# Running the second half of a gated embedding behind the last expert, tile by tile

## The chip, the cores and the metric

The kernel runs on one core of one Trainium2 chip. The metric is the device time of one execution in microseconds (us); a kernel's time is the median of its runs. Five engines work side by side: PE (matmuls, with PEld for the loads of its stationary operand), DVE, ACT, POOL and SP. SP issues nearly all weight loads. POOL issues the transfers that gather, scatter or add, on a queue of its own. The order of work on each engine is fixed when the program is built.

## The reference, cut to what matters

Two layers; each ends with a mixture of experts, a gated embedding and a layer norm. S is 512 rows, D_MODEL 1024, D_EXPERT 256, 16 experts, of which each row uses two.

```python
def hier_moe(h, ...):
    ...                                   # gates: (512, 16), two nonzeros a row
    a = jnp.einsum('td,edf->tef', t, w1)
    c = jnp.einsum('td,edf->tef', t, w3)
    act = jax.nn.silu(a) * c * gates[:, :, None].astype(t.dtype)
    y = jnp.einsum('tef,efd->td', act, w2)
...
    for i in range(DEPTH):
        ...
        h = layer_norm(DN_ALPHA * h + mix, ln1_g[i], ln1_b[i])
        y_moe = hier_moe(h, ...)
        y_ple = jax.nn.sigmoid(h @ ple_wg[i] + ple_bg[i]) * (p[i] @ ple_wp[i])
        h = layer_norm(DN_ALPHA * h + y_moe + y_ple, ln2_g[i], ln2_b[i])
```

## The kernel before

All matrix products are made of three matmuls: each operand is split in a high part (a cast on ACT, line 224) and a low part (a subtraction on DVE, line 225), and `mm3` adds high by high, low by high and high by low. Weights are streamed as a list of units in the order of use (`plan`). A unit is up to 128x1024 floats (0.52 MB): its raw tile is loaded by SP (line 240), then split, then used. `pump` loads some units ahead and splits a few ahead (`ahead_raw`, `ahead_split`: 15 and 3 in the expert stage, 7 and 3 from expert 10 on, 8 and 4 for the last expert). Raw and split tiles come from one set of 34 slots.

The 512 rows stand in four tiles of 128. After the first layer norm each tile goes to DRAM twice: to `hd`, from which experts gather their rows, and to `yd`, to which all that is to be added is added by accumulating transfers. An expert e takes four units for its two input products (`e<-whi,xT`), then a Silu (line 1274), a product, two transposes, a split of the activations (`actT`), and two units for its output (`e<-whi,actT`). The output units of expert e stand behind the input units of expert e + 1. The result is scaled by the gate into one of two places (`ye`, line 1323) and scattered into `yd` by POOL (line 1257). Experts 14 and 15 are treated apart: their results stay in SBUF as high and low parts (`yl`, lines 1315 and 1316), and one-hot matmuls (`hotT`, line 1431) bring them to their rows in the tail.

The gated embedding has a product of 1024 by 1024 (`ple_wg`) and one of 256 by 1024 (`ple_wp`, kept as `pwp`). Its first 512 columns are computed before expert 0. The second 512 columns take four units of weights, `pl<-...`, 24 matmuls each; two units run behind expert 3 and two behind expert 12 (`PLE_AT`). Each column half ends as bias sum (line 1206), tanh (line 1207) and product with `pwp` (line 1208), and is added into `yd` by POOL (line 1228).

The tail of a layer: POOL loads the four tiles of `yd` back (`h<-yd`, line 1412). `tail_sum` adds the one-hot products (on DVE, line 1437, or, for the tiles in `ZPE`, through an identity matmul and ACT, lines 1434 and 1435) and takes the row sums; then come the mean (line 362), the squares (line 364), the root on POOL (lines 305 and 308) and the two steps of the norm (lines 348 and 350, or 334 and 336). In the first layer each normed tile is transposed and split into `hT`, and the next layer's first projections (`pj`) start on it; in the second layer it is stored as output.

## Time and profile before

| | |
|---|---|
| median of 3 runs | 1043.53 us (1042.79 to 1048.24) |
| profiled execution | 1045.37 us, of which the trace spans 1043.6 |
| busy: PE, PEld | 968.6 us (93%), 800.6 us (77%) |
| busy: DVE, ACT, POOL | 779.1 (75%), 613.6 (59%), 172.9 (17%) |
| moved by DMA | 197.49 MB, 189 GB/s over the span |

The trace is of one execution. PE's busy time overstates its load, since matmuls overlap: a matmul of 512 columns has a duration of 0.39 us, but at full pace one starts every 0.23 us. PEld is the better measure of PE's pace. Clock times below are microseconds from the start of the span; the first layer's experts run from about 341 to 522, the second layer's from about 834 to 1016.

### The profile page before, as it was taken

What the parts mean: (1) busy time and instruction counts of PE and PEld (TensorE: products, weight loads), DVE (VectorE), ACT (ScalarE), POOL (GpSimd) and SP (SyncE); (2) the same over time, 40 slices, a digit from 0 to 9 for tenths busy, and PEclk for the clock granted to TensorE, in tenths of its full rate; (3) what the DMA queues carried; (4) which work ended last, traced back from release to release, by engine and by line L of the source; (5) the groups of instructions that cost most, each with busy time, mean ns of one, the idle gap of its engine ahead of it and who ended that gap; (6) DMA issues with size and microseconds to landing.
All of it is one profiled execution on the core that took longest, in us unless ns stands there. A gap on an engine that the chain in (4) does not pass through costs nothing. (4 is left out here: it accounts for less than half of the span.)

```text
span 1043.6 us, 14416 instructions
## 1 busy us (share of the span) xinstructions
PE 968.6 (93%) x4869; PEld 800.6 (77%) x4870; DVE 779.1 (75%) x1301; ACT 613.6 (59%) x1046; POOL 172.9 (17%) x170
## 2 busy tenths in 40 slices
PE   4999999999989999999979999999998999999995
PEld 3887889898767788777758889898776778877762
DVE  7576897777676778887865578847678587888785
ACT  5425464655653768886843346654655386888673
POOL 1101000000222222422121000000012222333121
PEclk9999999999999999999989999999999999999997
DMA  8816121222974999999974412122186399999974
GB/s 262 239 37 142 51 71 52 71 81 68 316 242 102 306 302 311 307 292 301 285 261 114 109 56 67 51 70 83 61 302 243 94 329 302 315 300 312 293 207 161
DMA packets 156010, 197.49 MB, mean 189 GB/s; under 512 B 20296, under 2 KB 123786, under 8 KB 155925
## 3 DMA queue, kind: packets, MB, share of 16 engines
q1 hardware_dynamic: 135253, 155.58, 45.5%
q0 software_dynamic: 20672, 40.87, 15.1%
q8 instruction: 42, 0.69, 0.3%
q14 instruction: 43, 0.35, 0.1%
HBM read 182.85 MB, written 29.36 MB: 203 GB/s over the span
## 5 line engine op out<-in xcount | busy, mean ns | idle before, releaser
L225 DVE TENSOR_TENSOR wlo<-raw,whi 128x1024 fp32r<-128x1024 f32 (+2 forms) x278 | 324.1, 1182 | 66.0 <-ACT whi L224 61.1
L224 ACT CAST whi<-raw 128x1024 fp32r<-128x1024 f32 (+2 forms) x278 | 277.9, 1024 | 33.1 <-DMA raw<-in_moe_w_dram 13.9
L218 PE MATMUL e<-whi,xT 128*128 128x512 f32 x256 | 106.6, 416 | 2.7 <-ACT xT L224 1.8
L219 PE MATMUL e<-wlo,xT 128*128 128x512 f32 x256 | 103.7, 405 | 0.1
L220 PE MATMUL e<-whi,xT 128*128 128x512 f32 x256 | 101.8, 398 | 0.0
L218 PE MATMUL pj<-whi,hT 128*128 128x384 f32 x256 | 90.0, 352 | 2.3 <-ACT hT L224 1.8
L219 PE MATMUL pj<-wlo,hT 128*128 128x384 f32 x256 | 88.2, 345 | 0.3 <-DVE wlo L225 0.3
L220 PE MATMUL pj<-whi,hT 128*128 128x384 f32 x256 | 87.3, 342 | 0.6 <-DVE hT L225 0.5
L1257 POOL DMA_INDIRECT yd<-ye,rt_tok x28 | 53.1, 1895 | 187.2 <-ACT ye L1323 66.7
L868 ACT ACTIVATE prob<-sc,mx 128x512 f32<-128x512 f32 x64 | 43.7, 688 | 39.1 <-DVE mx L867 36.6
L308 POOL TENSOR_TENSOR ors<-rs_y,mhalf 128x4 f32<-128x4 f32 x8 | 8.5, 1057 | 335.3 <-DVE rs_y L307 335.3
L1251 POOL DMA_INDIRECT xe<-hd,rt_tok x32 | 48.8, 1525 | 91.4 <-PE tr L376 48.1
L218 PEld LDWEIGHTS e<-whi,xT 128*128 128x128 f32 x256 | 48.9, 191 | 12.9 <-ACT xT L224 2.2
L219 PEld LDWEIGHTS e<-wlo,xT 128*128 128x128 f32 x256 | 48.8, 191 | 11.4 <-DVE wlo L225 2.4
L220 PEld LDWEIGHTS e<-whi,xT 128*128 128x128 f32 x256 | 48.8, 191 | 10.0
L219 PE MATMUL e<-wlo,actT 128*128 128x512 f32 x128 | 51.6, 403 | 3.1 <-DVE wlo L225 3.1
L218 PE MATMUL mo<-whi,YT 128*128 128x512 f32 x128 | 53.2, 415 | 0.0
L218 PEld LDWEIGHTS pj<-whi,hT 128*128 128x128 f32 x256 | 48.9, 191 | 4.8 <-ACT hT L224 2.5
L219 PE MATMUL pl<-wlo,hT 128*128 128x512 f32 x128 | 51.4, 401 | 1.1 <-DVE wlo L225 1.1
L218 PE MATMUL pl<-whi,hT 128*128 128x512 f32 x128 | 50.8, 402 | 0.6 <-ACT whi L224 0.5
L218 PE MATMUL e<-whi,actT 128*128 128x512 f32 x128 | 47.8, 398 | 3.8 <-ACT whi L224 2.9
L218 PE MATMUL pj<-hT,whi 128*128 128x512 f32 x128 | 51.2, 404 | 0.0
(340 smaller groups left out, 2313.1 us busy)
## 6 DMA issues: line engine op xcount, KB each, us to landing
raw<-in_moe_w_dram SPq DMA_DIRECT2D x256, 256.0 KB
raw<-in_moe_w_dram SPq DMA_DIRECT2D x64, 512.0 KB
raw<-in_w_in_dram SPq DMA_DIRECT2D x96, 128.0 KB
raw<-in_w_in_dram SPq DMA_DIRECT2D x16, 512.0 KB
raw<-in_ple_wg_dram SPq DMA_DIRECT2D x16, 512.0 KB
raw<-in_w_out_dram SPq DMA_DIRECT2D x14, 512.0 KB
tabi<-c_tabi_dram POOLq DMA_DIRECT2D x8, 516.0 KB, 4.6
tabf<-c_tabf_dram POOLq DMA_DIRECT2D x8, 512.0 KB
```

The costliest lines, as they stand in the source:

```text
L218: mm(ps, a[0], b[0], start=start, stop=False)
L219: mm(ps, a[0], b[1], start=False, stop=False)
L220: mm(ps, a[1], b[0], start=False, stop=stop)
L224: self.nc.scalar.copy(hi, src)
L225: self.nc.vector.tensor_sub(lo, src, hi.bitcast(F32))
L308: nc.gpsimd.tensor_tensor(out, y, self.mhalf[:, :n], op=OP.pow)
L868: nc.scalar.activation(p[:, c], o, AF.Exp, bias=mx[:, c:c + 1], accum_out=sm[:, c:c + 1])
L1251: self.nc.gpsimd.indirect_dma_start(out=x, out_offset=None, in_=self.hd[:, :], in_offset=bass.IndirectOffsetOnAxis(ap=tok, axis=0), bounds ...
L1257: self.nc.gpsimd.indirect_dma_start(out=self.yd[:, :], out_offset=bass.IndirectOffsetOnAxis(ap=row, axis=0), in_=y, in_offset=None, bounds ...
```

## The change

The second half of the gated embedding leaves the two places among the experts and stands behind the output of expert 15. Its four units are first all split, and then each tile of rows runs through all four (24 matmuls), so that one tile after the other is done. Bias sum and tanh are made in the PSUM bank, and the product overwrites `pwp`; nothing of it goes through `yd`. `tail_sum` adds it to the loaded tile (DVE takes sum and row sum of the right half, ACT the row sum of the left half). Experts 14 and 15 are scattered like the others; the `yl`, `hotT` and `own` tiles, the one-hot matmuls and `ZPE` go. The `ye` places and the first half's `plz` tiles share two places (`out4`); `plz` leaves the 34 slots. The tail of tile 0 is issued behind the gating of tile 2.

```diff
+    def out4(self, shape, name):
...
+        return _view(self.slots.tile([128, n], F32, name=name, tag="out4", bufs=2), shape)
...
-    def ple_tile(self, t, c, z, bias, o):
+    def ple_tile(self, t, c, z, o):
         nc = self.nc
-        nc.vector.tensor_add(o, z, bias)
-        nc.scalar.activation(o, o, AF.Tanh, scale=0.5)
-        nc.vector.scalar_tensor_tensor(o, o, 1.0, self.pwp[c][t // 2][:, t % 2], op0=OP.add, op1=OP.mult)
+        g = z if c else o
+        nc.vector.tensor_add(g, z, self.bg[:, c * 512:(c + 1) * 512])
+        act = nc.scalar.activation(g, g, AF.Tanh, scale=0.5)
+        dve = nc.vector.scalar_tensor_tensor(o, g, 1.0, self.pwp[c][t // 2][:, t % 2], op0=OP.add, op1=OP.mult)
+        self.gated[c, t] = act.ins, dve.ins
...
+        def second(q):
+            def f(wp):
+                st["w"].append(wp)
+                if q < 3:
+                    yield 0.01
+                    return
+                for t in range(NT):
+                    ps = self.ps("pl")
+                    for n, x in enumerate(st["w"]):
+                        mms(ps, t, n, x)
+                    self.ple_tile(t, c, ps, self.pwp[c][t // 2][:, t % 2])
+                    yield 5.12
+            return f
...
-                if k == 1 and e >= NE - NL:
...
-                elif k == 1:
-                    y = self.slots.tile([128, 1024], F32, name="ye", tag="ye", bufs=2)
+                if k == 1:
+                    y = self.out4([128, 1024], "ye")
...
+            if t == 0:
+                for ins in self.gated[1, 2]:
+                    order.enter_context(self.tc.issue_after(ins))
+            else:
+                order.enter_context(self.behind())
+            nc.scalar.activation(self.s2([128, 512], "lnsq", BF16), h[:, :512], AF.Copy, accum_out=sums[:, 0:1])
+            nc.vector.scalar_tensor_tensor(h[:, 512:], h[:, 512:], 1.0, self.pwp[1][t // 2][:, t % 2], op0=OP.mult,
+                                           op1=OP.add, accum_out=sums[:, 1:2])
             self.sums[t] = self.moments(h, LN_EPS / ALPHA ** 2, sums)
...
-            if e in self.PLE_AT:
-                self.add_ple(i, 1, self.PLE_AT.index(e))
         self.add_expert_out(i, NE - 1)
+        self.add_ple(i, 1)
...
-            if e in self.PLE_AT:
-                self.fill(2)
         self.fill(2)
+        self.load_stream()
+        self.fill(4)
```

POOL, at the end of the second layer, before. Lines 1257, 1251 and 1412 are the scatter, the gather and the load of the tail:

```order
191 L1257 DMA yd<-ye,rt_tok_8442 512x1024
192 L1228 DMA yd<-plz 128x2x512 x2
193 L1257 DMA yd<-ye,rt_tok_8442 512x1024 x2
194 L1412 DMA h<-yd 128x1024 x4
195 L305 TENSOR_SCALAR rs_y<-lnvar 128x1
```

The same place after the change (the scatter is line 1265 there, the gather 1259, the load 1409):

```order
186 L1259 DMA xe<-hd,rt_tok_8386 128x1024
187 L1265 DMA yd<-ye,rt_tok_8386 512x1024
188 L1259 DMA xe<-hd,rt_tok_8386 128x1024
189 L1265 DMA yd<-ye,rt_tok_8386 512x1024 x5
190 L1409 DMA h<-yd 128x1024 x4
```

The two `plz` transfers are gone, and two more scatters stand ahead of the loads.

ACT, around the last expert of the second layer, before. Line 1274 is the last Silu, `actT` the split of its activations, line 1315 the `yl` of experts 14 and 15 (two halves each), line 364 the squares of tile 0:

```order
755 L224 CAST whi<-raw 128x1024 x4
756 L1274 ACTIVATE act<-e_10801 128x256
757 L224 CAST actT<-e_10881 128x256
758 L224 CAST whi<-raw 128x1024
759 L1315 ACTIVATE yl<-e_10857,rt_gate_8467 128x512
760 L1315 ACTIVATE yl<-e_10858,rt_gate_8467 128x512
761 L1315 ACTIVATE yl<-e_10887,rt_gate_8467 128x512
762 L1315 ACTIVATE yl<-e_10888,rt_gate_8467 128x512
763 L364 ACTIVATE lnsq,lnvar<-h,lnneg 128x1024
```

The same place after (Silu 1282, cast 226, `ye` 1320, tanh 1204, row sum 1423):

```order
767 L1282 ACTIVATE act<-e_10593 128x256
768 L226 CAST whi<-raw 128x1024
769 L1320 ACTIVATE ye<-e_10645,rt_gate_8409 128x512
770 L226 CAST whi<-raw 128x1024
771 L1320 ACTIVATE ye<-e_10646,rt_gate_8409 128x512
772 L226 CAST whi<-raw 128x1024
773 L226 CAST actT<-e_10679 128x256
774 L226 CAST whi<-raw 128x1024 x3
775 L1320 ACTIVATE ye<-e_10685,rt_gate_8409 128x512
776 L1320 ACTIVATE ye<-e_10686,rt_gate_8409 128x512
777 L1204 ACTIVATE pl<-pl 128x512 x3
778 L1423 ACTIVATE lnsq,lnsum<-h 128x512
```

The casts in rows 768 and 770 are of the last expert's output units, those in rows 772 and 774 of the four `ple_wg` units: one stands ahead of `actT`, three ahead of the last `ye`. In the first layer `actT` stands ahead of all four.

DVE, in the second layer's tail, before (line 1437 adds the one-hot product, 362 is the mean, 348 and 350 the norm):

```order
1119 L1316 SCALAR_TENSOR_TENSOR yl<-e_10857,rt_gate_8467,yl 128x512
1120 L1316 SCALAR_TENSOR_TENSOR yl<-e_10858,rt_gate_8467,yl 128x512
1121 L1316 SCALAR_TENSOR_TENSOR yl<-e_10887,rt_gate_8467,yl 128x512
1122 L1316 SCALAR_TENSOR_TENSOR yl<-e_10888,rt_gate_8467,yl 128x512
1123 L1437 SCALAR_TENSOR_TENSOR h,lnsum<-h,el 128x512 x2
1124 L362 TENSOR_SCALAR lnneg<-lnsum 128x1
1125 L348 SCALAR_TENSOR_TENSOR ln<-h,lnneg,gain 128x512 x2
1126 L350 SCALAR_TENSOR_TENSOR h<-ln,lnrs,gain 128x512 x2
1127 L362 TENSOR_SCALAR lnneg<-lnsum 128x1
```

and after (1203 and 1205 are bias sum and product, 1424 the sum of the tail):

```order
1101 L1203 TENSOR_TENSOR pl<-pl,bg 128x512
1102 L1205 SCALAR_TENSOR_TENSOR pwp<-pl,pwp 128x512
1103 L1424 SCALAR_TENSOR_TENSOR h,lnsum<-h,pwp 128x512
1104 L364 TENSOR_SCALAR lnneg<-lnsum 128x1
1105 L350 SCALAR_TENSOR_TENSOR ln<-h,lnneg,gain 128x512 x2
1106 L352 SCALAR_TENSOR_TENSOR h<-ln,lnrs,gain 128x512 x2
1107 L1203 TENSOR_TENSOR pl<-pl,bg 128x512
1108 L1424 SCALAR_TENSOR_TENSOR h,lnsum<-h,pwp 128x512 x2
1109 L1205 SCALAR_TENSOR_TENSOR pwp<-pl,pwp 128x512
```

The first tail waits behind the gating of tile 2, and the gating of tile 3 stands between the tails of tiles 0 and 1.

## Rows read from the trace of the kernel before

**Rows 1.** The page's span, and DMA busy in 40 slices (tenths).

```profile
span 1043.6 us, 14416 instructions
DMA  8816121222974999999974412122186399999974
```

**Rows 2.** Windows: length; busy of PE, PEld, DVE, ACT, POOL; clock, DMA, GB/s.

```profile
380.00:390.00 10.00, 10.00 (x45) 8.12 (x44) 7.60 (x10) 3.15 (x4) 1.60 (x1) 1.00 0.79 243
...
870.00:880.00 10.00, 10.00 (x45) 8.18 (x44) 7.65 (x10) 4.87 (x6) 1.58 (x1) 1.00 0.86 273
...
1000.00:1010.00 10.00, 9.27 (x40) 6.82 (x39) 7.52 (x8) 7.20 (x9) 1.79 (x2) 1.00 0.79 268
```

**Rows 3.** Timeline, ACT: Silu of experts 3, 9, 10, 12, 15, second layer.

```profile
865.35 0.38 ACT L1274 ACTIVATE act<-e 128x256 f32<-128x256 f32 x1 [0.94 <-PE e L220]
...
934.88 0.39 ACT L1274 ACTIVATE act<-e 128x256 f32<-128x256 f32 x1 [0.40 <-PE e L220]
945.03 0.39 ACT L1274 ACTIVATE act<-e 128x256 f32<-128x256 f32 x1 [2.32 <-PE e L220]
...
967.25 0.38 ACT L1274 ACTIVATE act<-e 128x256 f32<-128x256 f32 x1
...
1010.00 0.38 ACT L1274 ACTIVATE act<-e 128x256 f32<-128x256 f32 x1
```

**Rows 4.** Waits, 830 to 1016: us in total, times, longest.

```profile
SPq L240 <- DMA raw<-in_moe_w_dram: 43.6, 67, 2.6
...
ACT whi L224 <- DMA raw<-in_moe_w_dram: 7.2, 7, 2.4
```

**Rows 5.** DMA, 840 to 1010: packets, MB, share; scatters, us to landing.

```profile
q1 hardware_dynamic: 32608, 44.05, 76.6%
q0 software_dynamic: 4445, 8.06, 19.6%
...
yd<-ye,rt_tok POOLq DMA_INDIRECT x14, 9.4
```

**Rows 6.** Timeline, PE: two matmuls of 512 columns that follow each other.

```profile
992.55 0.39 PE L219 MATMUL e<-wlo,xT 128*128 128x512 f32 x1
...
992.78 0.39 PE L220 MATMUL e<-whi,xT 128*128 128x512 f32 x1
```

**Rows 7.** Product (DVE) and tanh (ACT) of a 128x512 tile: ns min/median/max.

```profile
L1208 DVE SCALAR_TENSOR_TENSOR plz<-plz,pwp x16: 681/686/694, 330.1 to 986.1; 128x512 f32<-128x512 f32 x16
L1207 ACT ACTIVATE plz<-plz x16: 629/632/637, 329.1 to 985.4; 128x512 f32<-128x512 f32 x16
```

**Rows 8.** Timeline, the end of the second layer.

```profile
1008.79 2.13 POOL L1257 DMA_INDIRECT yd<-ye,rt_tok  x1 [8.21 <-ACT whi L224]
...
1013.44 1.27 ACT L1315 ACTIVATE yl<-e,rt_gate 128x512 fp32r<-128x512 f32 x2
...
1015.89 3.39 PE L1431 MATMUL el<-yl,hotT 128*128 128x512 f32 x11
1016.18 2.22 POOL L1412 DMA_DIRECT2D h<-yd  x4 [5.26 <-DVE yl L1316]
...
1020.66 0.69 DVE L1437 SCALAR_TENSOR_TENSOR h<-h,el 128x512 f32<-128x512 f32 x1 [2.86 <-DMA h<-yd]
...
1038.27 1.41 DVE L350 SCALAR_TENSOR_TENSOR h<-ln,lnrs,gain 128x512 f32<-128x512 f32 x2 [0.82 <-POOL lnrs L308]
```

**Rows 9.** Timeline, from the first layer's last scatter to the fourth `hT` tile.

```profile
517.77 1.58 POOL L1257 DMA_INDIRECT yd<-ye,rt_tok  x1 [8.50 <-DMA raw<-in_w_in_dram]
...
522.39 0.86 PE L1431 MATMUL el<-yl,hotT 128*128 128x512 f32 x3
...
525.18 1.83 POOL L1412 DMA_DIRECT2D h<-yd  x3 [5.83 <-DMA raw<-in_w_in_dram]
...
532.58 0.69 DVE L1437 SCALAR_TENSOR_TENSOR h<-h,el 128x512 f32<-128x512 f32 x1 [3.69 <-DMA h<-yd]
...
561.94 1.28 DVE L225 TENSOR_TENSOR hT<-tr,hT 128x512 fp32r<-128x512 f32 x2
```

More of the change, by code (lines that the diff above doesn't have):

```diff
@@ L1212, in add_ple @@
+    def add_ple(self, i, c):
         nc = self.nc
         cs = slice(c * 512, (c + 1) * 512)
[L1214 to L1229 removed]
@@ L1231, in emit, with mms, first @@
-        def emit(q):
+        st = {"w": []}
+        def mms(ps, t, q, wp):
+            for k in range(2):
+                self.mm3(ps, [x[:, q * 2 + k, t * 128:(t + 1) * 128] for x in self.hT],
+                         [x[:, k] for x in wp], q == 0 and k == 0, q == 3 and k == 1)
+        def first(q):
             def f(wp):
-                if q == qs[0]:
+                if q == 0:
                     st["ps"] = [self.ps("pl") for _ in range(NT)]
                 for t in range(NT):
-                    for k in range(2):
-                        self.mm3(st["ps"][t], [x[:, q * 2 + k, t * 128:(t + 1) * 128] for x in self.hT],
-                                 [x[:, k] for x in wp], q == qs[0] and k == 0, q == qs[-1] and k == 1)
-                    if q == qs[-1]:
-                        evac(t, st["ps"][t])
+                    mms(st["ps"][t], t, q, wp)
+                    if q == 3:
+                        if t % 2 == 0:
+                            self.plz[t // 2] = self.out4([128, 2, 512], "plz")
+                        z = self.plz[t // 2]
+                        self.ple_tile(t, c, st["ps"][t], z[:, t % 2])
+                        if t % 2:
+                            nc.gpsimd.dma_start(
+                                self.yd[(t - 1) * 128:(t + 1) * 128, cs].rearrange("(t p) n -> p t n", p=128), z,
+                                accum_op=OP.add)
@@ L1241, in f @@
                     yield 1.28
             return f
-        for q in qs:
+        def second(q):
[11 more added lines that the diff above has]
+            return f
@@ L1245, in add_ple @@
+        for q in range(4):
             src = self.A["ple_wg"][i][q * 256:(q + 1) * 256, cs].rearrange("(k p) n -> p k n", p=128)
-            self.add([(lambda r: r, src)], [2, 512], emit(q))
+            self.add([(lambda r: r, src)], [2, 512], (first, second)[c](q))
     def gather(self, tok):
@@ L1424, in tail_sum @@
         sums = self.sm.tile([128, 2], F32, name="lnsum", bufs=4)
-        with self.behind():
-            for c in range(2):
-                cs = slice(c * 512, (c + 1) * 512)
-                ps = self.ps("el")
-                for e in range(NE - NL, NE):
-                    for x in range(2):
-                        nc.tensor.matmul(ps, self.hotT[e][:, t], self.yl[e][x][:, cs], start=(e == NE - NL and x == 0),
-                                         stop=(e == NE - 1 and x == 1 and t not in self.ZPE[i]))
-                if t in self.ZPE[i]:
-                    nc.tensor.matmul(ps, self.ident, h[:, cs], start=False, stop=True)
-                    nc.scalar.activation(h[:, cs], ps, AF.Copy, accum_out=sums[:, c:c + 1])
-                    continue
-                nc.vector.scalar_tensor_tensor(h[:, cs], h[:, cs], 1.0, ps, op0=OP.mult, op1=OP.add,
-                                               accum_out=sums[:, c:c + 1])
+        with contextlib.ExitStack() as order:
+            if t == 0:
[6 more added lines that the diff above has]
+                                           op1=OP.add, accum_out=sums[:, 1:2])
             self.sums[t] = self.moments(h, LN_EPS / ALPHA ** 2, sums)
@@ L1609, in layer @@
             pass
-        self.xe, self.xT, self.act, self.actT, self.yl, self.hotT, self.plz = {}, {}, {}, {}, {}, {}, {}
+        self.xe, self.xT, self.act, self.actT, self.plz = {}, {}, {}, {}, {}
+        self.gated = {}
         self.ahead_raw, self.ahead_split = self.P_MOE
```

41 lines of the change are left out of this document (1 added, 40 removed).

## The prediction, made before the changed kernel ran

> **What bounds the kernel now.** I read the page first, for where the engines and the transfers are full, then the expert stage in windows, its pace by the Silu rows, who waits, and last the two tails row by row. In the forty slices DMA stands at 9 almost throughout both expert stages and falls away between the layers and at the end [rows 1]. So the expert stage is short of transfer time, and the tails have it to spare. SP's largest wait in the second stage is for its own earlier loads, 43.6 us in 67 waits; ACT waits 7.2 us for weights [rows 4]. The Silu rows show how this comes about. Once the embedding's first two units behind expert 3 are past, experts follow each other at 10.15 us (934.88 to 945.03); that is the engines' pace, and no load is waited for. It uses weights faster than they land, and the stock that was loaded ahead runs out near expert 12. From expert 12 to 15, with two embedding units between, 42.75 us pass [rows 3], and loads are waited for. The embedding's places inside the stage act as pauses: while PE works on them, the full set of slots lets DMA fall to 0.79 and 0.86 of its time [rows 2].
>
> **The change, part by part.** I call T0 the start of the first matmul behind the last expert's output: 522.39 in the first layer, 1015.89 in the second [rows 8, 9]. Three terms make the sum: how much earlier T0 comes, and how much longer each of the two tails gets.
>
> *The stage gets shorter (A).* Out of the stage go 96 matmuls a layer. At one per 0.23 us [rows 6] that is 22.1 us of PE. But if loads set the stage's end, only what leaves the transfer queues counts. Over 840 to 1010 the load queue took 76.6% of 170 us for 44.05 MB, or 2.96 us per MB, and POOL's queue 19.6% for 8.06 MB, or 4.13 us per MB [rows 5]. The four `ple_wg` units, 2.10 MB, now load behind the last expert's: 6.2 us. The two accumulating `plz` transfers of the second half, 1.05 MB, vanish: 4.3 us. The two scatters that are added come behind the last expert and cost the stage nothing. The pauses lose about 1 us in the second layer (0.86 in 10 us, where 0.96 is the stage's mean) and 2 us in the first (0.79) [rows 2, 5]. That makes 11.5 us in the second layer and 12.5 in the first; I take 12 there, since a pause is not wholly won back. Bounds: at least the weights' 6.2 us; at most 22, when the engines' pace holds to the end (expert 15 at 865.35 + 12 x 10.15 = 987.2 instead of 1010.0, 22.8 us [rows 3]). I take a value near the lower end, since 42.75 us for the last stretch, against 30.5 for three experts at pace and 11 for two units, shows loads already holding it back with the weights that now leave.
>
> *The second layer's tail (C).* Before, T0 to the end of the span is 1043.6 - 1015.9 = 27.7 us [rows 1, 8]. After, ACT takes the cast of the first `ple_wg` unit ahead of the last expert's activations. A unit of 0.52 MB lands 1.55 us behind the one before it, of which I take 1.3 as delay (bounds 0 and 2.6). Then PE runs the embedding; three of its matmuls stand ahead of the last expert's, in a gap (-0.7). Tile 2 is through after 72 matmuls, 16.6 - 0.7 = 15.9, and gated 2.2 us later (two DVE steps of 0.69, tanh 0.63, hand-overs [rows 7]): 18.1. Only then may the tail of tile 0 start. From there to DVE's last step it was 1020.66 to 1039.68, 19.0 us, in which the four norms follow each other [rows 8]. In the new order DVE has three more half-row sums less one, and the gating of tile 3: 2.75 us more. Against that PE and ACT no longer make sums through matmuls between the tiles; walking the new order step by step with the durations above I get 18.6. The last store takes 3.9 as before (1039.68 to 1043.6). Together 1.3 + 18.1 + 18.6 + 3.9 = 41.9, so C = +14.2. The removed one-hot matmuls earn nothing here beyond that: they ran while the tail waited for `h`.
>
> *Are the loaded rows in time?* The scatters go one after the other. The last before took 1008.79 to 1016.18 until the loads could be issued, 7.4 us, and the first load 4.5 more [rows 8]. Expert 14's result was out at 1014.71, T0 - 1.2, so two scatters end at T0 + 13.6 and tile 0 is there at 18.1, just in time. In the first layer, where the next layer's weights load meanwhile, both the scatter (517.77 to 525.18) and the load (to 532.58) took 7.4 [rows 9]: T0 + 21.0. The median scatter in the full stage takes 9.4 [rows 5], which is the upper bound for each of the three steps; the lower is 4.5.
>
> The Trainium skill, DMA: Bandwidth & Descriptors, section Anatomy of one DMA, gives 2.0 us plus bytes over 436 GB/s for one such transfer. By it an estimate for scatters of 0.26 MB (half of an expert's 128 rows are taken on the mean) and a load of 0.52 MB is 2.6 + 2.6 + 3.2 us, the rows would be there by T0 + 8, and the sum below would be 1.1 us less. The rows above, two to three times that, disagree, and I go by them.
>
> *The first layer's tail (B).* What counts is when the fourth tile's `hT` is written and the next layer's projections are free. Before, that is 563.22 (561.94 + 1.28), T0 + 40.8 [rows 9]. After, `actT` is not held by a cast, but the four `ple_wg` units need 6.2 us behind the last expert unit, and tile 0 wants the fourth earlier; I take 1.8 us of delay (bounds 0 and 6.2). Tile 2 is gated at 18.1 + 1.8 = 19.9, `h` arrives at 21.0. From the first sum to the last `hT` it was 30.6 (532.58 to 563.22); by the new order I get 29.3, for the same reasons as in C. 21.0 + 29.3 - 40.8 = +9.5. Upper bound, three steps of 9.4: `h` at 27.0, +15.5.
>
> *Edits at nothing:* the shared places `out4`. `plz` is written before expert 0 and its transfer has about two experts at pace, 20 us, to land; without that cover the first `ye` would wait up to the 9.4 us that such a transfer of POOL's takes [rows 3, 5]. The slots that `plz` frees cost nothing and only help A. Bias sum and tanh in PSUM instead of SBUF keep their count and size.
>
> **Sum.** -12 + 9.5 in the first layer, -11.5 + 14.2 in the second: +0.2 us. Against the profiled execution, 1045.37 us, that is 1045.6; the median of the runs is 1.8 lower, so I predict 1044. Half a percent, 5.2 us, is about what a measurement of this kernel can tell from no change.
>
> **The rivals.** (1) *Loads don't bind, faster.* With the pauses gone DMA might run fuller than 0.96, or the stock last longer, and T0 come some 17 us earlier in each layer: 23.7 - 34 = -10, about 1033. For it: the engines' pace of 10.15 leaves 22.8 us of room in the stage [rows 3], and part of the waits for loads fell in the stretches in which the embedding's own weights were among them. Against it: DMA share is at 9 in nearly every slice of the stage, and SP's wait is for its own loads. It decides from A above 14.5 on the mean.
>
> (2) *The rows come late, slower.* Two more scatters in a row hold the loads back, as one mechanism: POOL waits for each before the next. At 9.4 each, `h` comes at 27.0 in the first layer (+6.0) and, with two at 9.4 and a load of 4.5, at 22.1 in the second (+4.0): +10, about 1054. For it: the queue is fuller then, with `ple_wg` and the next layer's weights behind the experts'. Against it: in the second layer nothing more loads after these. It decides from a mean scatter above 8.5 us.
>
> (3) *Only the weights count, slower.* If the accumulating transfers take bandwidth that was not lacking, and no pause is won back, A is 6.2 in each layer: 23.7 - 12.4 = +11, about 1055. For it: in the last window of the stage DMA is at 0.79 [rows 2]. Against it: by queue time the two kinds take turns at the same 96%.
>
> (4) *The gain and the loss hide*, which is my forecast with other sizes; that the change does not do what it says I see no way for, since the order shows it.
>
> **How the numbers follow.** My forecast, within 5.2 us of no change, 0.46; rival 1 0.20; rival 2 0.20; rival 3 0.13; 0.01 is left for anything else. So faster 0.20, same 0.46, slower 0.34. The likeliest case's own range is 1039 to 1049, from A between 10 and 14 a layer. To leave out no more than 2 in 10 the range goes to 1034 on the side of rival 1 and to 1055 on that of rivals 2 and 3.
>
> **What the changed profile would show.** A right: the Silu of expert 15 about 11 to 12 us earlier, with more ACT waits for expert weights from expert 9 or 10 on, and DMA at 0.95 or more to the stage's end; wrong if spacings stay at 10.15 (rival 1) or the last Silu is only 6 earlier (rival 3). C right: the last DVE step about 38 us behind the first embedding matmul there; and the first tail sum right behind tile 2's product, not behind a load. B right: the fourth `hT` some 50 us behind T0. A wait of the first tail sum for `h<-yd` of more than 2 us is rival 2. What would make all wrong: a stall of ACT or DVE, which are filled in order, on a cast whose weights have not landed, earlier in the stage than I looked.

## The result, and the profile after

The changed kernel takes 1050.07 us (median) against 1043.57 us for the kernel before, measured beside each other: a ratio of 1.0068, 95% interval 1.0054 to 1.0082. A second measurement (experiment `a_again`) gave 1.0033, interval 1.0008 to 1.0058. By these two ratios the change makes the kernel 0.3 to 0.7% slower; between the means of all runs it is 5.8 us (1043.4 over 114, 1049.2 over 29). One execution of the changed kernel, of 2379.87 us, is left out of means and ratios. The two measurements of the changed kernel differ by 2.7 us in their means (standard error 1.2), so prices of a few us are read below with that in mind.

Both kernels were profiled twice, so each term of the prediction can be read from two executions. T0 is again the first matmul behind the last expert's output; in the changed kernel that is an embedding matmul.

| stretch, us | forecast | before | changed | mean change |
|---|---|---|---|---|
| start to first Silu, layer 1 | 0 | 345.24, 346.15 | 344.84, 344.56 | -1.0 |
| first Silu to T0, layer 1 (A) | -12 | 177.15, 174.26 | 166.70, 167.22 | -8.7 |
| T0 to the fourth `hT` (B) | +9.5 | 40.83, 41.56 | 51.26, 48.02 | +8.4 |
| fourth `hT` to first Silu, layer 2 | 0 | 274.90, 276.21 | 280.02, 279.63 | +4.3 |
| first Silu to T0, layer 2 (A) | -11.5 | 177.77, 178.22 | 168.64, 168.68 | -9.3 |
| T0 to the span's end (C) | +14.2 | 27.71, 27.30 | 39.64, 39.69 | +12.2 |
| span | +0.2 | 1043.6, 1043.7 | 1051.1, 1047.8 | +5.8 |

The page of the first changed profile: the span, the granted clock and DMA busy in 40 slices (tenths), to be laid beside [rows 1].

```profile
span 1051.1 us, 14219 instructions
...
PEclk9999999999989999998989999999999899998997
DMA  8815121232974999999755221222295499999952
```

The stage still runs with DMA at 9. Three pieces of the trace show what became of it. First ScalarE's timeline, second layer: the Silu of experts 9, 11, 12 and 15, which answer to [rows 3], and its wait for weights over 830 to 1016, which answers to [rows 4].

```profile
931.62 0.38 ACT L1282 ACTIVATE act<-e 128x256 f32<-128x256 f32 x1 [0.39 <-PE e L222]
...
952.98 0.39 ACT L1282 ACTIVATE act<-e 128x256 f32<-128x256 f32 x1 [0.66 <-PE e L222]
968.06 0.38 ACT L1282 ACTIVATE act<-e 128x256 f32<-128x256 f32 x1
...
999.69 0.38 ACT L1282 ACTIVATE act<-e 128x256 f32<-128x256 f32 x1 [0.60 <-PE e L222]
```

```profile
ACT whi L226 <- DMA raw<-in_moe_w_dram: 8.7, 9, 4.9
```

Without the embedding's units the engines' pace of 10.15 us holds to expert 10 (21.4 us for two experts from 931.62 on), then the stock of weights is empty and one expert takes 15.1 us (952.98 to 968.06), 5 above the pace, with a single wait of 4.9. From expert 12 to 15 it is 31.6 us where it was 42.75: the 11 us of two units come back whole, but of the like saving at expert 3 the stall gives 5 away. Then TensorE's timeline at that stall in the first layer (idle time before an instruction stands in brackets at its end):

```profile
468.14 0.40 PE L222 MATMUL e<-whi,actT 128*128 128x512 f32 x1
473.42 1.22 PE L220 MATMUL e<-whi,actT 128*128 128x512 f32 x2 [4.88 <-ACT whi L226]
...
475.26 0.63 PE L222 MATMUL e<-whi,actT 128*128 128x512 f32 x1
475.69 0.63 PE L221 MATMUL e<-wlo,actT 128*128 128x512 f32 x1
```

Behind 4.88 us of idleness matmuls of 512 columns follow each other in 0.43 us, not in the 0.23 of [rows 6]: TensorE is at the lower of its two levels. The prediction's sum has full clock throughout.

The second layer's end, from the timelines of ScalarE, TensorE, POOL and VectorE (answers to [rows 8]). First the line of the kernel before at which TensorE starts on the last expert's output, behind the Silu at 1010.00:

```profile
1012.64 0.50 PE L218 MATMUL e<-whi,actT 128*128 128x512 f32 x1 [0.46 <-ACT actT L224]
```

Then the changed kernel, where that Silu is at 999.69:

```profile
1004.96 1.04 ACT L226 CAST whi<-raw 128x1024 fp32r<-128x1024 f32 x1 [0.62 <-DMA raw<-in_ple_wg_dram]
1005.90 0.36 ACT L226 CAST actT<-e 128x256 fp32r<-128x256 f32 x1
...
1006.32 0.50 PE L220 MATMUL e<-whi,actT 128*128 128x512 f32 x1 [3.91 <-ACT actT L226]
...
1011.46 0.39 PE L220 MATMUL pl<-whi,hT 128*128 128x512 f32 x1
...
1019.27 2.24 POOL L1409 DMA_DIRECT2D h<-yd  x4 [5.07 <-DVE pwp L1205]
...
1029.53 0.68 DVE L1424 SCALAR_TENSOR_TENSOR h<-h,pwp 128x512 f32<-128x512 f32 x1
...
1045.84 1.40 DVE L352 SCALAR_TENSOR_TENSOR h<-ln,lnrs,gain 128x512 f32<-128x512 f32 x2
```

The last expert's `actT` stands behind the cast of `ple_wg`, TensorE waits 3.91 us for it where it waited 0.46, and from the last Silu to T0 it is 11.8 us instead of 5.9. From T0 on the forecast holds: the first sum at T0 + 18.1, right behind tile 2's product and not behind a load, and VectorE's last step ends 17.7 us later.

The first layer's tail (answers to [rows 9]):

```profile
508.99 1.55 POOL L1265 DMA_INDIRECT yd<-ye,rt_tok  x1 [7.99 <-ACT whi L226]
...
518.26 1.55 POOL L1265 DMA_INDIRECT yd<-ye,rt_tok  x1 [7.72 <-DMA raw<-in_w_in_dram]
526.62 0.60 POOL L1409 DMA_DIRECT2D h<-yd  x1 [6.81 <-DVE wlo L227]
...
511.54 0.39 PE L220 MATMUL pl<-whi,hT 128*128 128x512 f32 x1
...
533.85 0.69 DVE L1424 SCALAR_TENSOR_TENSOR h<-h,pwp 128x512 f32<-128x512 f32 x1 [3.59 <-DMA h<-yd]
...
561.51 1.29 DVE L227 TENSOR_TENSOR hT<-tr,hT 128x512 fp32r<-128x512 f32 x2 [1.50 <-ACT hT L226]
```

The last two scatters took 9.3 and 8.4 us, by the spacing to what POOL issued next, and the first sum waits 3.59 us for `h`, T0 + 22.3. In the second profile (`a_again`) they took 9.1 and 7.1 us, and the sum waits 1.81 us.

### The profile page after: what moved, and what is told of

Its sections match the earlier page's. It is cut to its first block, busy times and chain, and to the rows that moved or that the text cites. A ratio compares the mean times of both kernels' runs of the same rounds, so it can differ in the third digit from the quotient of the medians.

```text
span 1051.1 us, 14219 instructions
## 1 busy us (share of the span) xinstructions
PE 959.3 (91%) x4789; PEld 792.5 (75%) x4790; DVE 767.5 (73%) x1279; ACT 613.7 (58%) x1046; POOL 172.6 (16%) x170
## 3 DMA queue, kind: packets, MB, share of 16 engines
q0 software_dynamic: 20160, 39.91, 14.4%
## 5 line engine op out<-in xcount | busy, mean ns | idle before, releaser
L221 PE MATMUL e<-wlo,xT 128*128 128x512 f32 x256 | 106.5, 416 | 2.9 <-DVE wlo L227 2.7
L1265 POOL DMA_INDIRECT yd<-ye,rt_tok x32 | 57.9, 1809 | 226.0 <-ACT ye L1320 144.3
L220 PE MATMUL pj<-whi,hT 128*128 128x384 f32 x256 | 91.3, 358 | 1.7 <-ACT hT L226 1.1
L222 PE MATMUL pj<-whi,hT 128*128 128x384 f32 x256 | 88.4, 346 | 0.0
L220 PE MATMUL e<-whi,actT 128*128 128x512 f32 x128 | 48.0, 409 | 16.6 <-ACT whi L226 11.7
L1320 ACT ACTIVATE ye<-e,rt_gate 128x512 f32<-128x512 f32 x64 | 43.5, 688 | 27.1 <-PE e L222 26.9
```

Of the source, the lines that this page charges most:

```text
L220: mm(ps, a[0], b[0], start=start, stop=False)
L221: mm(ps, a[0], b[1], start=False, stop=False)
L222: mm(ps, a[1], b[0], start=False, stop=stop)
L1265: self.nc.gpsimd.indirect_dma_start(out=self.yd[:, :], out_offset=bass.IndirectOffsetOnAxis(ap=row, axis=0), in_=y, in_offset=None, bounds ...
L1320: nc.scalar.activation(y[:, c * 512:(c + 1) * 512], st["ps"][c], AF.Copy, scale=self.gates[:, e:e + 1])
```

## The experiments

Twelve kernels ran. Each is timed against the kernel before on the same chip; the stretches named are those of the table.

**The same two kernels again.** No edit.

> The kernel before, unchanged, once more. In the two profiles at hand, the changed kernel needs 280.0 us from the end of the fourth hT of the second layer's input (562.80) to the first Silu of the second layer's experts (842.82), the kernel before 274.9 (563.22 to 838.12), though the change moves no instruction there. Theory 'clock': that stretch differs from execution to execution with the places at which the granted clock falls to its lower level, so this profile gives some other value between 273 and 279 and other places. Rival 'fixed': the value belongs to the kernel, and it comes out at 274.9 within 0.5 again, with falls at the same places.

> The changed kernel, unchanged, once more. Theory 'clock': the stretch from the fourth hT to the first Silu of the second layer takes something between 274 and 281 us, with the granted clock low at places that the first profile does not show; the waits of the two tails (T0 to the fourth hT 51.3, T0 to the span's end 39.6) are the same within 1 us. Rival 'fixed': 280.0 within 0.5 us, low clock at the same places as before (740 to 750, 770 to 775, 820 to 830).

Measured: before 0.9995 (0.997 to 1.002) of itself; fourth `hT` to first Silu 276.2 in it and 279.6 in the changed kernel. The places at which the clock fell moved (before: from 783 and 813, then from 742 and 787; changed: from 743, 768 and 818, then from 740, 785 and 815). T0 to the end repeated within 0.05 in the changed kernel; T0 to the fourth `hT` did not repeat within 1 us (51.3, 48.0), a miss of that line. The stretch depends on where the clock falls, but its mean for the changed kernel stayed high in both. Over all kernels here it runs from 274.8 to 280.0, and the time lost to the lower clock in it (its length by 1 less its mean granted clock) is 1.7 to 6.8; a straight line through the 14 profiles gives 0.9 us of time for 1 us so lost (correlation 0.75). That is not all of it: where 5.1 us are lost, the three profiles of the kernel before and its variants have 275.8 to 276.2, the three of the changed kernel and its variants 278.1 to 279.6. What makes those 2 to 4 us is not shown.

**The late rows** (the last two scatters are left out).

```diff
-                    self.scatter(y, self.rows[:, e:e + 1])
+                    if e < NE - 2:
+                        self.scatter(y, self.rows[:, e:e + 1])
```

> Left out: the scatters of the last two experts of each layer, so their results are missing from the output; the loads of h then wait for expert 13's scatter alone. This prices the late rows. In the changed kernel the first tail sum of the first layer waits 3.6 to 4.2 us for h behind tile 2's product, in the second layer not at all. Theory 'rows cost only that wait': the first sum comes right behind tile 2's product in both layers (T0 + 18.7), the first layer's tail gets 3 to 4 us shorter, the second layer's does not change, and the time falls by 3 to 4 us, to some 1046.5. Rival 'rows late is the main loss' (rival 2 of the prediction with its whole 10 us): the time falls by 8 us or more. Rival 'nothing': less than 1.5 us, since the tail's pace is set by the four norms and the clock.

Measured: 1044.97 us, ratio 1.0023 (1.0002 to 1.0044), 3.5 under `a_again` by the medians, 1.9 by the means (standard error 1.3). VectorE's timeline, first layer: product of tile 2, then the first sum with nothing between.

```profile
528.36 0.69 DVE L1205 SCALAR_TENSOR_TENSOR pwp<-pl,pwp 128x512 f32<-128x512 f32 x1 [0.65 <-ACT pl L1204]
528.96 0.68 DVE L1425 SCALAR_TENSOR_TENSOR h<-h,pwp 128x512 f32<-128x512 f32 x1
```

T0 to the fourth `hT` is 46.9 where it was 48 to 51, T0 to the end 39.67 as before. The rows cost 1 to 4 us in the first layer and nothing in the second: the expectation with the small price.

**Behind the last expert: weights or order?** Fewer loads (one unit used four times), and casts ahead only by 2.

```diff
-                st["w"].append(wp)
...
+                st["w"] = [wp] * 4
...
+            if c and q:
+                continue
```

> Left out: three of the four weight loads of the embedding's second half in each layer; the one that is loaded is used four times with the same count of matmuls, so that half of the embedding is wrong in value. This prices the loads behind the last expert. Theory 'loads bind' (the prediction's 2.96 us per MB): 1.57 MB less is up to 4.7 us a layer, of which 3 to 4.7 should show as an earlier end of the embedding's first tile against the last Silu; the time falls by 6 to 9 us, to 1041 to 1044. Rival 'the engines set it': the casts and matmuls of the last experts pace that stretch, the first tile comes less than 1.5 us earlier a layer, and the time falls by under 3 us.

```diff
-    P_LAST = 8, 4
+    P_LAST = 8, 2
```

> Nothing is left out. Casts are made 2 units ahead in place of 4 from the last expert on, which takes the cast of the embedding's first unit from ahead of the last expert's activations on ScalarE. In both profiles of the changed kernel the second layer needs 11.8 us from the last Silu to T0, where the kernel before needed 5.9: the cast of ple_wg waits for its load, and actT stands behind it (1004.96, then 1005.90). Theory 'order': 11.8 falls to 7 to 9 us, and the time by 3 to 4 us; in the first layer, where the weights land in time (7.0 against 6.6), nothing changes. Rival 'loads': the weights themselves are late, so that the embedding's first tile comes no earlier against the last Silu, and the time changes by under 1 us.

Measured: `a_1w` 1046.80, ratio 1.0029 (1.0009 to 1.0049), last Silu to T0 7.1 and 11.3 (6.9 and 11.7 in `a_again`): behind the last expert the three further loads, and the casts that go with them, are worth nothing, the rival's result. `a_split` 1049.45, ratio 1.0045 (1.0025 to 1.0065): last Silu to T0 fell from 11.7 to 9.5, as the order theory had it in kind but less than its 7 to 9, and T0 to the end grew from 39.7 to 42.8. TensorE still waits for `actT`, which now stands behind one cast and the two halves of expert 14's `ye`:

```profile
1001.54 0.50 PE L220 MATMUL e<-whi,actT 128*128 128x512 f32 x1 [1.88 <-ACT actT L226]
```

Why the tail grew VectorE's timeline tells: with the casts late, TensorE takes the tiles side by side, weight by weight, and they are all done at the end. These are the bias sums of tiles 0 to 2, at T0 + 14.3 and every 2.6 us, where the changed kernel has them from T0 + 5 on every 5.5.

```profile
1020.75 0.70 DVE L1203 TENSOR_TENSOR pl<-pl,bg 128x512 f32<-128x512 f32 x1 [10.08 <-PE pl L222]
...
1023.31 0.70 DVE L1203 TENSOR_TENSOR pl<-pl,bg 128x512 f32<-128x512 f32 x1 [0.52 <-PE pl L222]
...
1025.86 0.70 DVE L1203 TENSOR_TENSOR pl<-pl,bg 128x512 f32<-128x512 f32 x1 [0.51 <-PE pl L222]
```

**What binds the stage.** The look-ahead uncut in the changed kernel; then, in the kernel before, two thirds of the second half's matmuls left out, and half of its loads left out.

```diff
-    P_END = 7, 3
+    P_END = 15, 3
```

> Nothing is left out. The look-ahead of the loads stays at 15 units from expert 10 on, where the changed kernel cuts it to 7. In the changed kernel ScalarE waits for expert weights ahead of expert 12 (11.5 us in the first layer, 7.5 in the second), and TensorE loses its full clock there. Theory 'rate' (the prediction's: transfers bind from the moment when the stock is used up): the stall moves to a later expert, but the last Silu comes no more than 1.5 us earlier, since the bytes are the same. Rival 'cut': loads that could have been under way are held back by the cut; the stall goes, and the last Silu comes 4 us or more earlier in each layer, the time falls by 6 to 10 us.

```diff
+                    if part is None:
...
+                    else:
+                        nc.tensor.matmul(st["ps"][t], self.hT[0][...], wp[0][:, 0], start=q == qs[0], stop=False)
+                        nc.tensor.matmul(st["ps"][t], self.hT[0][...], wp[1][:, 0], start=False, stop=q == qs[-1])
```

> The kernel before with two thirds of the second half's matmuls left out (32 of 96 a layer are kept, 14.7 us of TensorE fewer), all loads and transfers as they were, so that half of the embedding is wrong in value. It asks what TensorE's part was worth in the stage. Theory 'loads bind': the pauses alone are won back, first Silu to T0 gets 1 to 2 us shorter a layer, the time falls by 2 to 4 us. Rival 'engines': most of the 14.7 us come back, 8 us or more a layer.

```diff
+        def both(wp):
+            for q in qs:
+                yield from emit(q)(wp)
...
+            return self.add([(lambda r: r, src)], [2, 512], both)
```

> The kernel before with half of the second half's weight loads left out (two of four units, 1.05 MB a layer): each unit that is loaded is used for both of its pair, with the same count of matmuls, so that half of the embedding is wrong in value. It asks what weights are worth in the stage by themselves. Theory 'loads bind' (the prediction's 2.96 us per MB): first Silu to T0 gets 3.1 us shorter in each layer (from 175.7 on the mean of two profiles in the first, 178.0 in the second), the time falls by 5 to 7 us. Rival 'engines': less than 1 us a layer, time within 2 us.

Measured: `a_pend` 1054.72, ratio 1.0103 (1.0062 to 1.0144): first to last Silu 160.6 and 158.4 (160.3 and 156.9 in `a_again`), so a longer look-ahead gains nothing, and last Silu to T0 12.4 in the first layer instead of 7. `b_lessmm` 1043.71, ratio 0.9997 (0.9979 to 1.0015): first Silu to T0 176.0 and 177.6, unchanged. Spacing of the Silu in the second layer shows where 14.7 us of TensorE went:

| us from expert to expert | 3 to 4 | 9 to 10 | 10 to 11 | 11 to 12 | 12 to 13 | 1 to 15 |
|---|---|---|---|---|---|---|
| before (second profile) | 20.5 | 10.2 | 11.2 | 11.4 | 22.6 | 164.3 |
| `b_lessmm` | 14.4 | 10.1 | 11.9 | 14.9 | 19.2 | 163.9 |
| `b_halfwg` | 20.5 | 10.1 | 11.2 | 9.4 | 20.6 | 158.7 |
| changed (second profile) | 9.9 | 10.1 | 11.2 | 16.0 | 11.4 | 149.2 |

What expert 3 saves, experts 11 to 15 give back waiting for weights: loads bind. ScalarE's waits for expert weights in the second layer's stage grow from 7 us to 10.8. TensorE's granted clock is lower here (0.9748 on the mean of the runs, 0.9796 before), and by the time that goes with the clock over the runs of the kernel before (last section) some 3 us of gain may be hidden in that, but not the rival's 8 a layer. `b_halfwg` 1039.51, ratio 0.996 (0.994 to 0.998): 5.6 us less from first Silu to T0 in the second layer for 1.05 MB, where I had 3.1, but 177.5 in the first layer, no gain at all. Two units' casts and splits go with the loads, some 2.0 us of ScalarE and 2.4 of VectorE, less than the 5.6. ScalarE's waits for expert weights tell the two apart: in the second layer they fall from 7 us to 1.9, in the first they stay at 7.0.

**One part alone: no accumulating transfers.** In the kernel before.

```diff
+        p = self.pwp[c][t // 2][:, t % 2]
...
-        nc.vector.scalar_tensor_tensor(o, o, 1.0, self.pwp[c][t // 2][:, t % 2], op0=OP.add, op1=OP.mult)
+        nc.vector.scalar_tensor_tensor(p if c else o, o, 1.0, p, op0=OP.add, op1=OP.mult)
...
-                if t % 2:
+                if t % 2 and c == 0:
                     nc.gpsimd.dma_start(self.yd...
...
+                if c:
+                    nc.tensor.matmul(ps, self.ident, self.pwp[1][t // 2][:, t % 2], start=False,
+                                     stop=t not in self.ZPE[i])
```

> The kernel before with one part of the change alone: the second half of the embedding stays at its places behind experts 3 and 12, but its product stays on the chip and is added in the tail through a matmul with the identity (0.59 us each, two in the path at most), so that its two accumulating transfers (1.05 MB a layer) vanish. Nothing is left out. Theory of the prediction ('transfers bind, 4.13 us per MB'): each layer's stage gets 4.3 us shorter from its first Silu to T0 (177.8 in the second layer's two profiles of the kernel before), the tails 0.6 to 1.2 longer, the time falls by 6 to 8 us, to 1035 to 1037. Rival 3 of the prediction ('only weights count'): the stage does not change, and the time is within 2 us of the kernel before.

Measured: 1032.76, ratio 0.988 (0.9851 to 0.9908): faster than both kernels, and for another reason than the expected one. First Silu to T0 is 174.3 and 176.9, hardly shorter. T0 to the fourth `hT` is 35.3 (41.2 before), T0 to the end 25.4 (27.5). POOL's timeline at the first layer's end, first in the kernel before (second profile):

```profile
491.47 1.32 POOL L1228 DMA_DIRECT2D yd<-plz  x1 [10.29 <-DVE plz L1208]
493.88 1.19 POOL L1228 DMA_DIRECT2D yd<-plz  x1 [1.08 <-DVE plz L1208]
505.41 2.14 POOL L1257 DMA_INDIRECT yd<-ye,rt_tok  x1 [10.34 <-DMA yd<-plz]
516.12 1.58 POOL L1257 DMA_INDIRECT yd<-ye,rt_tok  x1 [8.57 <-DMA raw<-in_w_in_dram]
523.32 1.83 POOL L1412 DMA_DIRECT2D h<-yd  x3 [5.62 <-DVE wlo L225]
```

and in `b_noplz`, with the first one-hot matmul (T0) and the first sum:

```profile
497.78 1.84 POOL L1258 DMA_INDIRECT yd<-ye,rt_tok  x1 [16.35 <-ACT actT L224]
508.21 1.60 POOL L1258 DMA_INDIRECT yd<-ye,rt_tok  x1 [8.59 <-DMA raw<-in_w_in_dram]
516.08 1.82 POOL L1413 DMA_DIRECT2D h<-yd  x3 [6.26 <-DMA raw<-in_w_in_dram]
...
517.96 0.99 PE L1432 MATMUL el<-yl,hotT 128*128 128x512 f32 x3
...
523.13 0.69 DVE L1441 SCALAR_TENSOR_TENSOR h<-h,el 128x512 f32<-128x512 f32 x1 [0.16 <-DMA h<-yd]
```

The two transfers of `plz` keep the scatter behind them waiting 10.34 us (its row names them); by their spacing, 10.7 and 7.2 us, the next scatter and the loads of `h` go one at a time behind it, so they come later too, and the first sum with them. Without them the loads go out 1.9 us ahead of T0 instead of 2.9 behind it, and the sum comes at T0 + 5.2 instead of 9.8.

**The clock.** Matmuls without use in the gaps of the changed kernel: first in the first layer's tail alone, then in all gaps over 3 us of its first profile.

```diff
+                    if i == 0 and t == NT - 1:
+                        warm = self.ps("warm")
+                        for _ in range(18):
+                            nc.tensor.matmul(warm, self.hT[0][:, 0, 0:128], st["w"][3][0][:, 0], start=True, stop=True)
```

> Added: 18 matmuls without use (4.2 us at full clock) behind the embedding's fourth tile in the first layer, in the gap in which TensorE waits for the first norm. In the changed kernel's profiles the granted clock then falls to 0.59 to 0.73 over 535 to 545. Theory 'clock': with TensorE busy up to the transposes the clock stays at 1.00 up to the fourth hT, T0 to the fourth hT falls from 48 to 51 us by 2 to 4, and the time with it. Rival 'norms': the stretch is paced by the four norms on VectorE and ScalarE, the clock stays high and nothing comes earlier (within 1 us), or the transposes come later by what the added matmuls overhang (1 to 2 us longer).

```diff
+                for _ in range({(0, 11, 1): 14, (1, 11, 1): 14, (0, 15, 0): 4, (1, 15, 0): 15}.get((i, e, k), 0)):
+                    nc.tensor.matmul(self.warm, self.hT[0][:, 0, 0:128], self.hT[0][:, 0], start=True, stop=True)
```

> Added: matmuls without use in all the gaps in which the changed kernel's TensorE waits for more than 3 us: 14 ahead of expert 11's last two halves (weights), 15 in the second layer and 4 in the first ahead of the last expert's output (actT), 18 in the first layer behind the embedding. Over the runs so far the mean granted clock is 0.979 for the kernel before (58 runs) and 0.970 for the changed one (29 runs), and within each kernel's runs 0.01 of clock goes with some 6 us. Theory 'clock': the waits themselves are covered, but each is followed by 5 to 10 us at the lower clock, in which TensorE is what the chain waits for; filled, the mean clock comes to 0.976 or more and the time falls by 3 to 6 us against the changed kernel. Rival 'covered': what follows the gaps is paced by loads and norms, so a slow TensorE costs nothing there; the clock rises, but the time stays within 1.5 us of the changed kernel's.

Measured: `a_warm` 1046.26, ratio 1.0033 (1.0015 to 1.0051); `a_fill` 1046.20, ratio 1.0024 (1.0004 to 1.0043). Windows of 10 us in the changed kernel (length, then busy time of PE, PEld, DVE, ACT, POOL, then granted clock, DMA share, GB/s): the stall of the first layer, its tail twice, the stall of the second layer, the wait for `actT`.

```profile
470.00:480.00 10.00, 6.54 (x22) 4.79 (x23) 4.90 (x5) 6.44 (x9) 1.58 (x1) 0.66 0.98 335
530.00:540.00 10.00, 5.75 (x26) 4.48 (x25) 5.42 (x12) 3.18 (x8) 0.75 (x2) 0.82 1.02 370
540.00:550.00 10.00, 8.05 (x38) 6.80 (x38) 8.92 (x17) 6.56 (x15) 2.66 (x4) 0.84 0.01 3
...
965.00:975.00 10.00, 6.76 (x23) 4.96 (x24) 5.11 (x5) 6.65 (x9) 1.79 (x1) 0.66 0.95 321
1000.00:1010.00 10.00, 6.09 (x23) 4.68 (x22) 6.99 (x9) 7.84 (x10) 1.58 (x1) 0.87 0.71 183
```

The same places in `a_fill` (its second layer runs some 10 us earlier):

```profile
470.00:480.00 10.00, 7.37 (x28) 5.42 (x27) 5.48 (x7) 6.28 (x8) 1.58 (x1) 0.83 0.96 327
530.00:540.00 10.00, 8.62 (x42) 6.89 (x41) 7.75 (x17) 5.60 (x12) 1.27 (x3) 1.00 0.90 324
540.00:550.00 10.00, 8.56 (x51) 7.77 (x51) 8.93 (x15) 5.57 (x13) 3.35 (x6) 1.00 0.01 2
...
955.00:965.00 10.00, 7.59 (x33) 5.69 (x32) 4.39 (x6) 4.51 (x6) 0.00 (x0) 1.00 0.88 297
990.00:1000.00 10.00, 9.44 (x41) 7.04 (x41) 7.26 (x9) 7.45 (x10) 1.70 (x1) 1.00 0.69 193
```

The mean granted clock over the runs for which it is on record is 0.9796 before (94 runs), 0.9700 changed (29) and 0.9791 in `a_fill` (12), and the mean times are 1043.4, 1049.2 and 1046.0. Keeping TensorE busy with nothing gives back 3.2 of the 5.8 us (standard error 0.9), at the low end of the 3 to 6 expected; against the ten runs of `a_again` alone it is 1.4 (1.2), so the size is uncertain. The last Silu to T0 falls from 11.7 to 9.9. In the first layer's tail `a_warm` seems to come out as its rival said: clock 1.00 there, and T0 to the fourth `hT` 48.5, no shorter than in `a_again` (48.0). But the rows came later in it. These are its first sum and the end of its fourth `hT`:

```profile
531.18 0.69 DVE L1428 SCALAR_TENSOR_TENSOR h<-h,pwp 128x512 f32<-128x512 f32 x1 [3.19 <-DMA h<-yd]
...
556.54 1.29 DVE L227 TENSOR_TENSOR hT<-tr,hT 128x512 fp32r<-128x512 f32 x2 [1.50 <-ACT hT L226]
```

From the first sum on it takes 26.7 us, and the same in `a_fill`, against 29.0 and 27.6 in the two profiles of the changed kernel, in which the granted clock over that stretch is 0.82 and 0.88. So 0.9 to 2.3 us came back there, less than the theory's 2 to 4 and hidden by a later `h` (T0 + 21.8, where `a_again` had 20.5). Part of it may be VectorE's order, in which the fourth tile's bias sum moved ahead.

**Rows early again, tails between the tiles.** One-hot matmuls for the last two experts as before, `h` loaded during the last expert, each tail issued two tiles behind its own.

```diff
+        self.work(1)
+        self.work(1)
+        self.last = None
+        self.tail_sum(i, 0)
+        self.work(1)
+        self.ln_tile(0, 0 in self.APART[1])
+        self.tail_sum(i, 1)
+        self.work(1)
```

> Undoes one part of the change and regroups the tail: the last two experts' rows go through one-hot matmuls again, h is loaded while the last expert runs, and the tail of tile 0 is issued behind the embedding's second tile, that of tile 1 behind the third; the embedding's product is added through a matmul with the identity. Nothing is left out. Theory 'the tail is long because rows and norms start late': the first sum comes at T0 + 12 to 14 in place of T0 + 18 to 22, T0 to the fourth hT takes 36 to 42 us in place of 48 to 51, T0 to the span's end 32 to 35 in place of 39.6, and the time falls by 12 to 20 us, below the kernel before (1028 to 1038). Rival 'the scatters are not the cost': the embedding's 22 us and the four norms stand in a row anyway, less than 5 us come back, and the kernel stays at 1044 or more.

Measured: 1058.20, ratio 1.0131 (1.0114 to 1.0148), a clear miss. The first sum did come at T0 + 12.0 in the second layer, but T0 to the end took 47.0, and T0 to the fourth `hT` in the first layer 55.5. TensorE's timeline at the second layer's end:

```profile
1030.66 1.09 PE L1449 MATMUL el<-yl,hotT 128*128 128x512 f32 x4
1031.58 1.02 PE L1454 MATMUL el<-h,cst 128*128 128x512 f32 x2
1032.04 1.50 PE L1449 MATMUL el<-yl,hotT 128*128 128x512 f32 x4
1033.38 1.02 PE L1452 MATMUL el<-pwp,cst 128*128 128x512 f32 x2
1034.23 1.02 PE L1454 MATMUL el<-h,cst 128*128 128x512 f32 x2
```

These 4.6 us stand between tile 2 and tile 3 without a gap. With 5.5 us of embedding a tile needs 10 us of TensorE, and the tail that was bound by VectorE's norms is now bound by TensorE: over 1012 to 1059 its matmuls make 71% of the chain that ended last. In the second layer's tail of the kernel before the same one-hot matmuls ran where TensorE had nothing else to do.

## Why the prediction was right, point by point

The time lay 6 us above the forecast, within the range, on the side to which it gave 0.34. The first measurement (6.5 us by the medians) lies just past the 5.2 us that the prediction calls no change and past the 1049 of its likeliest case, the second (4.7 us) inside both. The mechanism (stage shorter, two tails longer, near balance) is what the traces show. That the sum came so near is in part luck: A was 3.3 and 2.2 us short, B and C came 1.1 and 2.0 us better than forecast, and 3.3 us came in stretches that had no term.

*A, forecast -12 and -11.5, measured -8.7 and -9.3.* The failed step is "the two accumulating `plz` transfers of the second half, 1.05 MB, vanish: 4.3 us". `b_noplz` takes these away, at the price of identity matmuls in the tails: the stage gets 1.4 and 1.1 us shorter, the first within what the two profiles of the kernel before differ there (2.9), the second beyond it (0.5). The price of 4.13 us per MB was the queue's busy time, and what those transfers cost stands elsewhere: in the row of stores on POOL ahead of the loads of `h`. The change put two scatters in their place there, so that it could not win what `b_noplz` wins. The Trainium skill, Trainium Kernel Development and Optimization, section Key Constraints, says that transfers of all queues share 16 engines and interleave; at a DMA share of 0.96 that suggests that the bytes count in the stage. Here a megabyte on POOL's queue was worth about 1 us of it, and the measurement decides. Without this term A would have been -7.7 and -7.2, nearer to what came at T0, but 1 to 2 too small.

In the second layer that nearness is luck. Read by the last Silu, before `actT` comes into it, the stage is 9.2 us shorter in the first layer and 15.2 in the second, of which 5.9 is lost again between the last Silu and T0 (under C). So the weights' 6.2 us was too small there: `b_halfwg` gave 5.6 us for half of those bytes, with the casts that go with them. In the first layer it gave nothing, since ScalarE's waits for expert weights stayed as they were; why they did is open, and with it what a megabyte of weights is worth. A at T0, 9.0 on the mean, lies below the 10 to 14 of the likeliest case.

That loads bind, on which A rested, is shown: `b_lessmm` frees 14.7 us of TensorE a layer and gains nothing, and `a_pend` shows that the cut of the look-ahead is not what starves the stage. Rival 1, with A above 14.5 at T0, is out by the table. Rival 3 (A = 6.2) was as near in size as the forecast, and right about the accumulating transfers.

*C, forecast +14.2, measured +12.2.* The parts held: first sum at T0 + 18.1 (forecast 18.1), the norms to VectorE's end 17.7 (18.6), the store 3.9 (3.9). The step that failed is the delay of `actT`, "of which I take 1.3 as delay (bounds 0 and 2.6)": last Silu to T0 grew by 5.9, outside the bounds, and it lies ahead of T0, so it counts in A and not in C. By `a_split` 2.2 of it go with the cast of `ple_wg`, the only thing that the step had in it. The rest had no term: expert 14's `ye`, whose counterpart `yl` stood behind `actT` before, now stands ahead of it, TensorE takes three embedding matmuls in between (the 0.7 that the forecast took off behind T0), and the matmuls behind the wait run at 0.43 us for a while. These three are read from order and trace and were not priced one by one.

*B, forecast +9.5, measured +8.4 on the mean.* Tile 2 was gated at T0 + 18.7, `h` came at T0 + 22.3 and 20.5 (forecast 21.0), the fourth `hT` at 51.3 and 48.0 (50.3). That `h` came when forecast is luck as well. The forecast starts expert 14's scatter at T0 - 1.2, when its result was out, though by [rows 9] expert 13's held the queue until T0 + 2.8; from there three steps of 7.4 end at T0 + 25.0. In the changed kernel the scatter of expert 14 went out at T0 - 2.5. No `plz` transfers stood ahead of expert 13's there, and in `b_noplz`, too, expert 13's ends 4.7 us earlier against T0. In turn the steps were longer than 7.4 on the whole: 9.3, 8.4 and 7.2. Rival 2's marks are half there: the first sum waits 3.59 and 1.81 us for `h` (over 2 was its sign), and the two scatters take 8.8 and 8.1 us on the mean in the first layer, 7.2 in the second (over 8.5 was its sign). Its mechanism was in the forecast already, and `a_noscat` prices the whole of it at 1.9 to 3.5 us, not 10.

*What had no term.* The sum has TensorE at full clock everywhere. In the first layer's tail TensorE waits for rows or a norm in both kernels (3.7 and 4.7 us before, 4.3 and 2.5 in the changed one), but the changed one has further waits, at expert 12 and for `actT`: 4.9, 4.1 and 3.9 us in its first profile, 3.5 and 3.9 in its second. Matmuls at 0.43 us follow them. The Trainium skill, TensorE: Matmul & The Clock Gate, section HAM oscillation — how this bites in real kernels, tells of this: a wait for a transfer also makes what follows it start slowly. The trace agrees (0.43 us behind 4.88 us of idleness), and `a_fill` prices it at 3.2 us over all runs, 1.4 against `a_again` alone. The table's terms without the stretches that the change does not touch give 2.6, and `a_fill` is 2.6 above the kernel before; that is chance in part, since some of the clock's price lies inside A, and does not show that the balance closes. The rest of the 5.8 us lies in a stretch that the change does not touch: from the fourth `hT` to the next layer's first Silu the seven profiles of the changed kernel and its variants without filling show 276.0 to 280.0, the two with filling 274.8 and 276.3, the five of the kernel before and its variants 274.9 to 276.2. How a wait in one place could make the clock fall 200 us later these runs do not tell, nor whether it does, and at the same loss of clock the changed kernel and its variants are still 2 to 4 us slower there. This part of the cause stays open.

From the windows of [rows 2] I had 1 to 2 us for the pauses, and `b_lessmm` no gain; both are too small to be told apart here.

## What to carry to other kernels

The share of time that a queue's packets take is not what its bytes cost: find the wait that the transfer ends last. Here 1.05 MB of accumulating transfers a layer cost about 1 us in the stage full of transfers, and 8 us in the two tails together, because the next loads stand behind them on their queue; leaving them out, with identity matmuls in their place, made a kernel 1.2% faster than before. Work that TensorE did here under a stage bound by loads was nearly free (`b_lessmm`) and kept its clock up; moved behind the stage, with the other edits, it made the two tails 8 and 12 us longer, and the stall that it had covered was paid for in waiting and, by `a_fill`, in half-speed matmuls behind the wait. Before casts, tails or tiles are reordered, look at what the order puts last on the other engines: `a_split` and `w_early` won part of what they were made for and lost more behind it. And compare a stretch from the event that starts it: `a_warm` seemed to gain nothing because its rows came later.

## What the runs showed of the hardware that was not expected

Two profiles of the changed kernel differ by 3.3 us in span, nearly all of it in the first layer's tail (51.3 and 48.0), 1.9 of it by when `h` came and 1.4 behind that: a single profile is worth no more than that. Over the runs 0.01 of mean granted clock goes with 6.0 us in the kernel before and 6.2 in the changed one. That is a going together, not a price: `a_fill` raised the mean clock by 0.009 and gained 1.4 to 3.2 us, not 5.5, and in the first layer's tail raising the clock from 0.82 and 0.88 to 1.00 gave 0.9 to 2.3 us in 27 to 29.
